# The scan's group statistics share the C.B bank, and the products' ring gets the bank set free

## The chip, the cores and the metric

The kernel runs on one core of a Trainium2 chip. The metric is the time of one execution in microseconds as the device counts it. The kernel before takes 2577.64 us, the median of three runs (2576.39 to 2583.05). The engines are called PE (TensorE, matmuls; PEld is its weight load), DVE (VectorE), ACT (ScalarE), POOL (GpSimd) and SP (SyncE, whose queue issues all the DMAs here). Each engine issues its own instructions in a fixed order and waits on semaphores for the others.

## The reference, cut to what matters

One layer of a streaming encoder works on 1088 tokens at once: 1024 of a new stream and 64 of a running one. The part around the change is this:

```python
xn = _rmsnorm(x, p['norm_mix_w'])
z, xbc, dt_raw, q, k, v, gate_ssm, gate_att = split(xn @ p['w_in'])
...
# the scan, chunk after chunk, 32 heads in 4 groups
cb = einsum('blgn,bsgn->blsg', cc, bc)
y = einsum('blsg,blsge,bsgep->blgep', cb, decay, xdt)
y = y + einsum('blgn,bgepn->blgep', cc, state) * exp(acum)
state = state * exp(acum[:, -1]) + einsum('blgn,blge,blgep->bgepn', bc, to_end, xdt)
...
y_ssm = (y + D * xs) * silu(z)
y_ssm = _rmsnorm(y_ssm per group, p['ssm_norm_w'])
o = diff_attention(q, k, v)
mix = sigmoid(gate_ssm) * (y_ssm @ w_branch_ssm) + sigmoid(gate_att) * (o @ w_branch_attn)
x = x + mix @ p['w_out']
x = x + conv_ffn(_rmsnorm(x))
```

## The kernel before, in words

Everything is kept transposed: features on the 128 partitions, tokens along the free axis. Tokens are cut in three columns of 384, 384 and 320 (`WIDE`). The stages follow each other: norm and values, q and k with their statistics, attention (with projections as filler), the scan (with projections and branches as filler), the rest of the branches, the output projection, the FFN.

**Products.** Every large matrix product runs in three passes over a high and a low part of both operands (`product`, lines 140 to 145), 24 matmuls for a product of eight k-tiles. The accumulator comes from `acc` (line 112), which hands out banks of PSUM in turn. During the first stage it turns over five banks, three of them from a pool that ends with that stage (`more`, line 226); from then on it has the two banks of the pool `pm`, tag "mm". A bank is free again when its reader has emptied it: for the branches that reader is the gate multiplication on VectorE (line 196, tile `b_g`). `project` (line 147) makes the tiles of the input projection; its accumulators are emptied by ScalarE. `branch` (line 156) makes a branch product: for each of the two halves of 544 tokens and each of eight output tiles it loads the gate and a weight tile, splits the weight in high and low (lines 136 and 137) and makes two products of 272 tokens. Where `stage` is given, it also loads the normed scan output in quarters (`b_f` from `y_sc`, line 168) and splits it into `b_hi` (ScalarE, line 169) and `b_lo` (VectorE, line 170). There are three branch calls: the attention's (768 matmuls), the scan's first two groups (768), and the scan's last two groups (768, after the scan).

**The scan.** It goes through 4 groups x 3 columns, 12 spans. A span has three steps of 128 tokens (the last step of the last column has 64). A step (`step`, from line 658) transposes x into `tr` (line 671), B and C.B into `cb` (lines 673 and 674), copies `cb` with ScalarE into `b_cb` (line 676), scales x on VectorE into `xdt` and `xw` (line 681), masks and exponentiates the decay on GpSimd and ScalarE (lines 682 and 684), multiplies it with C.B on VectorE (`bc`, line 685), and makes the within-chunk output `yi` (line 689), the carried-in output `ye` (line 696) and the state update `stp` (line 702). VectorE combines them (lines 697, 698 and 709). After a span's steps, `gated` adds D.x (line 718, VectorE), multiplies by the gate (line 719, GpSimd), squares (line 720, ScalarE), adds the four tiles up (lines 721 and 722, GpSimd), and one matmul with a matrix of ones sums over the partitions: the group sum, tile `gst` (line 724). From it `rstd_of` (lines 209 to 217) takes Ln and Exp on ScalarE and three more steps on VectorE, and line 728 scales y, which is then stored to `y_sc`.

**The banks in the scan.** PSUM has eight: two for `pm` ("mm"), and one each, with one buffer, for `tr`, `cb`, `yi`, `ye`, `stp` and `gst`. A tile of a one-buffer tag can be written only when all readers of the one before, in the program's order, are done.

**The order of the work.** The program is written as a scan that calls `fill` after each step and each `gated`: 2.5 filler units each time, first the rest of the input projection, from span 9 in the program's order on the branches. A scheduler that works with modelled durations then orders each engine's instructions before the program is built, so an instruction that would wait in the model is passed by later ones that would not, as far as buffers allow. What it decides is fixed on the chip.

Of the kernel before, what the change touches and what calls it, by code (L numbers as in the profile page):

```python
# [9 lines left out]
F32 = mybir.dt.float32  # L10
# [4 lines left out]
PSUM = bass.MemoryType.PSUM  # L15
DRAM = bass.MemoryType.DRAM

P = 128
# [58 lines left out]
def hybrid_layer(ctx: ExitStack, tc: tile.TileContext, xT, prm, cst, rope, wvd, win, wbs, wba, wout, wup, wdn,  # L77
# [27 lines left out]
    def col(o):  # L105
        return par[:, o : o + 1]

    pm = ctx.enter_context(tc.tile_pool(name="pm", bufs=2, space=PSUM))

    more, at_bank = None, 0  # L110

    def acc(w):
        nonlocal at_bank
        at_bank = (at_bank + 1) % 5
        pool, tag = (more, "mx") if more is not None and at_bank < 3 else (pm, "mm")
        t = pool.tile([P, 512], F32, name=tag, tag=tag)
        return t[:, :w]

# [28 lines left out]
    def project(block, evac):  # L147
        w_hi, w_lo = weights(block, KT, P)
        for c, w in WIDE:
            ps = acc(w)  # L150
            product(ps, [(w_hi[:, k], w_lo[:, k], xn_hi[:, k, c : c + w], xn_lo[:, k, c : c + w]) for k in range(KT)])
            with tc.high_priority(quick or ahead):
                evac(ps, c, w)
            yield

    def branch(stage, pair, src, wts, g0, add, out):
# [18 lines left out]
        for x, c in enumerate((0, HALF)):  # L175
            hi, lo = parts[x]
            if x == 0:
                parts[1] = octet()
            for m in range(KT):
                r = slice(P * m, P * (m + 1))  # L180
                two = pair()
                gt, at = two[:, :HALF], two[:, HALF:T]
                first = load(out=gt, in_=g_sc[g0 + P * m : g0 + P * (m + 1), c : c + HALF])
                if add is not None:
                    load(out=at, in_=add[r, c : c + HALF])
                w_hi, w_lo = weights(wts[m], KT, P)
                if x == 0 and m >= LAG:
                    with tc.issue_after(first.ins):
                        for k in range(8 * (m - LAG) // (8 - LAG), 8 * (m - LAG + 1) // (8 - LAG)):
                            bring(HALF, k, *parts[1])  # L190
                for a in (0, HALF // 2):
                    q = slice(a, a + HALF // 2)
                    ps = acc(HALF // 2)
                    product(ps, [(w_hi[:, k], w_lo[:, k], hi[:, k, q], lo[:, k, q]) for k in range(KT)])
                    with tc.high_priority(ahead):
                        V.scalar_tensor_tensor(gt[:, q], gt[:, q], 1.0, ps, ALU.add, ALU.mult)  # L196
                if add is not None:
                    V.tensor_tensor(out=gt, in0=gt, in1=at, op=ALU.add)
                out(m, c, gt)
                yield  # L200
# [4 lines left out]
    def run(gen):  # L205
        for _ in gen:
            pass

    def rstd_of(pool, out, mean, w, tag, scale=1.0, top=384):
        t = [pool.tile([P, top], F32, name=f"{tag}{i}", tag=f"{tag}{i}") for i in range(2)]  # L210
        u, r = (x[: out.shape[0], :w] for x in t)
        act(u, mean, AF.Ln, bias=eps_t[: out.shape[0]], scale=scale)
        act(r, u, AF.Exp, scale=-0.5)
        V.tensor_scalar(u, mean, -0.5 * scale, -0.5 * EPS, ALU.mult, ALU.add)
        V.tensor_tensor(out=u, in0=u, in1=r, op=ALU.mult)
        V.tensor_tensor(out=u, in0=u, in1=r, op=ALU.mult)
        V.scalar_tensor_tensor(out, u, 1.5, r, ALU.add, ALU.mult)
# [5 lines left out]

    s1 = ExitStack()
    ps1 = s1.enter_context(tc.tile_pool(name="ps1", bufs=1, space=PSUM))
    more = s1.enter_context(tc.tile_pool(name="psx", bufs=3, space=PSUM))

    def stat(w):
        t = ps1.tile([P, 512], F32, name="st", tag="st", bufs=3)
        return t[:, :w]  # L230
# [4 lines left out]
    with tc.tile_pool(name="nx", bufs=1) as nx:  # L235
        S.preload_act_table_set(LN_EXP)
        c = 0
        for x, w in enumerate(NORM):
            xc = nx.tile([P, KT, max(NORM)], F32, name="xc", tag="xc", bufs=3)
            ps = stat(w)  # L240
# [25 lines left out]
    def values(f, dt=None, pools=(None, None)):  # L266
        m = 256 if dt is None else 272
        w2 = [weights(win[B_V + 2 * f - 4 + u] if dt is None else wvd[2 * f + u], 4, m, pools[u]) for u in range(2)]
        for i in range(9):
            n = min(P, T - i * P)  # L270
            ps = acc(m)[:n]
            product(ps, [(xn_hi[:, k, P * i : P * i + n], xn_lo[:, k, P * i : P * i + n],
                          w2[k // 4][0][:, k % 4], w2[k // 4][1][:, k % 4]) for k in range(KT)])
            vo = staged("vo")[:, :256]
            with tc.high_priority(quick or ahead):
                S.copy(vo[:n], ps[:, :256])
                if dt is not None:
                    V.tensor_tensor(out=dt[:n, i, 16 * f : 16 * f + 16], in0=ps[:, 256:],
                                    in1=par[:n, O_DTB + 16 * f : O_DTB + 16 * f + 16], op=ALU.add)
            load(out=v[P * i : P * i + n, 256 * f : 256 * (f + 1)], in_=vo[:n])  # L280
            yield
# [124 lines left out]
            split_out(ck, j, PAST, c_st)  # L406
        heads(B_K, lambda j: col(O_KN + j), k_st, kT)
    s1.close()
    more = None
    ahead = AHEAD  # L410
    extra.release()
    extra = None
# [225 lines left out]


    with tc.tile_pool(name="sp", bufs=1) as sp, tc.tile_pool(name="pss", bufs=1, space=PSUM) as pss:  # L640
        def fetch(g, c, w):
            t = sp.tile([P, 10, 384], F32, name="in", tag="in", bufs=2)
            four = slice(4 * P * g, 4 * P * (g + 1))
            for u in range(2):
                load(out=t[:, u, :w], in_=x_sc[P * (16 + 4 * u + g) : P * (17 + 4 * u + g), c : c + w])
            for u, d in ((2, x_sc), (6, z_sc)):
                load(out=t[:, u : u + 4, :w], in_=d[four, c : c + w].rearrange("(j p) t -> p j t", p=P))
            return t
# [65 lines left out]
        def gated(g, c, w, xs, zt, y):  # L714
            rows = slice(4 * P * g, 4 * P * (g + 1))
            part = lambda d: d[rows, c : c + w].rearrange("(j p) t -> p j t", p=P)
            for j in range(4):
                V.scalar_tensor_tensor(y[:, j], xs[:, j, :w], col(O_D + 4 * g + j), y[:, j], ALU.mult, ALU.add)
            G.tensor_tensor(out=y, in0=y, in1=zt, op=ALU.mult)
            act(zt, y, AF.Square)  # L720
            G.tensor_tensor(out=zt[:, 0:2], in0=zt[:, 0:2], in1=zt[:, 2:4], op=ALU.add)
            G.tensor_tensor(out=zt[:, 0], in0=zt[:, 0], in1=zt[:, 1], op=ALU.add)
            ps = pss.tile([P, 512], F32, name="gst", tag="gst")[:, :w]
            PE.matmul(ps, ones, zt[:, 0], start=True, stop=True)
            rs = sp.tile([P, 384], F32, name="grs", tag="grs", bufs=2)[:, :w]
            rstd_of(sp, rs, ps, w, "gn", 1.0 / 512)
            for j in range(4):
                V.scalar_tensor_tensor(y[:, j], y[:, j], col(O_SN + 4 * g + j), rs, ALU.mult, ALU.mult)  # L728
            load(out=part(y_sc), in_=y)

        def scan():
            spans = [(g, c, w) for g in range(4) for c, w in WIDE]
            raw = fetch(*spans[0])
            ready = [gate(raw, spans[0][2])]
            for i, (g, c, w) in enumerate(spans):
                if c == 0:
                    state = None
                if i + 1 < len(spans):
                    raw = fetch(*spans[i + 1])
                bx, xs, zt = ready[i]  # L740
                y = sp.tile([P, 4, 384], F32, name="y", tag="y", bufs=2)
                for o in range(0, w, P):
                    state, last = step(g, (c + o) // P, o, bx, xs, y, state)
                    if o == P * GATE_AT and i + 1 < len(spans):
                        ready.append(gate(raw, spans[i + 1][2], last))
                    yield i
                gated(g, c, w, xs, zt, y[:, :, :w])
                yield i
# [21 lines left out]
            fill(SCAN_STEPS)  # L770
        load(out=conv, in_=conv_o)
        run(filler)
    dq.release()


# [17 lines left out]
    with tc.tile_pool(name="op", bufs=1) as op:  # L793
        for c, w in WIDE:
# [3 lines left out]
            for m in range(KT):  # L798
# [4 lines left out]
                ps = acc(w)  # L803
# [9 lines left out]
            ps = psf.tile([P, 512], F32, name="st2", tag="st2")[:, :w]  # L813
# [12 lines left out]
    with tc.tile_pool(name="fq", bufs=1) as fq, tc.tile_pool(name="fp", bufs=1) as fp:  # L826
# [42 lines left out]
        for n in DOWN:  # L869
            hid = [hidden(k0 + i) for i in range(n)]  # L870
            for mp2 in range(4):
                o = 1024 * k0 + 256 * n * mp2
                w_hi, w_lo = weights(wdn[:, o : o + 256 * n], n, 256)
                for u in range(2):
                    m = 2 * mp2 + u
                    for c, w in WIDE:
                        ps = acc(w)
# [114 lines left out]
```

## Time and profile before

| what | value |
|---|---|
| median of three runs | 2577.64 us |
| the profiled execution's own time | 2582.58 us |
| its span in the trace | 2580.8 us |
| norm, values, q and k | 0 to 416 us |
| attention | 416 to about 1116 us |
| scan, first transposes to last group sum | 1116.8 to 1567.0 us |
| rest of the branches, output projection, FFN | to 2580.8 us |

A row of stretches gives a length and each engine's busy time in it, with the number of instructions; then the granted clock of TensorE (1.00 is full), the DMA engines' share and GB/s. A row of groups names line, engine, operation, output and inputs, the count, then busy time and the mean of one in ns, then the idle time of the engine just before them and what ended it. A row of waits says who waited for whom: total us, times, longest.

### The profile page before, as it was taken

How to read it: one execution, taken by the hardware profiler on the slowest of the kernel's cores; microseconds unless marked ns; L12 is line 12 of the kernel's file. 1: busy time of each engine (PE TensorE's matmuls, PEld its weight loads, DVE VectorE, ACT ScalarE, POOL GpSimd, SP SyncE). 2: the span in 40 equal slices, each digit the busy share in tenths (PEclk: the TensorE clock that was granted, in tenths of full speed). 3: DMA queues.
4: the chain of work that ended last, by engine and by line, in shares of the span. 5: the costliest groups of instructions: out<-in, count | busy, mean ns of one | idle time of the engine just before them, and what ended most of it. 6: DMA issues, size and time to landing. Idle time of an engine off the chain costs nothing.

```text
span 2580.8 us, 41810 instructions
## 1 busy us (share of the span) xinstructions
PE 2525.0 (98%) x16484; PEld 2444.8 (95%) x16484; DVE 1399.8 (54%) x2371; ACT 1032.2 (40%) x2113; POOL 290.0 (11%) x387
## 2 busy tenths in 40 slices
PE   8999999999999999999999989999999999999999
PEld 7999999999999999988788879999999999999999
DVE  7326266654447674665679997658333333343333
ACT  5334234544445554565456643335312222131221
POOL 3000001000001110022333430023000000000000
PEclk9999999999999999999999999999999999999999
DMA  5217167545435433176798978555311111111112
GB/s 162 83 54 282 51 257 213 153 142 148 131 126 164 136 112 111 64 232 192 245 332 258 304 246 272 195 187 193 119 42 47 44 42 50 42 50 40 44 43 77
DMA packets 233685, 366.59 MB, mean 142 GB/s; under 512 B 31184, under 2 KB 160464, under 8 KB 233360
## 3 DMA queue, kind: packets, MB, share of 16 engines
q1 hardware_dynamic: 233488, 363.91, 44.2%
q8 instruction: 130, 2.13, 0.3%
q14 instruction: 67, 0.55, 0.1%
HBM read 263.56 MB, written 100.27 MB: 141 GB/s over the span
## 4 chain that ended last, share of the span: by engine, by line
PE 43%; DMA 3%; DVE 3%; ACT 1%; issue 1%; SPq 0%; POOL 0%; DVEq 0%; ACTq 0%; POOLq 0%
PE mm L143 7%; PE mm L145 7%; PE mm L144 7%; PE up L143 7%; PE up L145 7%; PE up L144 7%; DMA in<-x_sc 1%; DMA b_hi<-o_sc 1%; DVE w_lo L137 1%; PE yi L689 1%; PE stp L702 0%; ACT bc L684 0%; DVE y L728 0%; DMA in<-z_sc 0%; DVE b_lo L170 0%
## 5 line engine op out<-in xcount | busy, mean ns | idle before, releaser
L143 PE MATMUL mm<-xn_hi,w_hi 128*128 128x320 f32 (+1 forms) x1496 | 497.9, 333 | 2.3 <-ACT zr L428 1.1
L145 PE MATMUL mm<-xn_hi,w_lo 128*128 128x320 f32 (+1 forms) x1496 | 496.8, 332 | 0.0
L144 PE MATMUL mm<-xn_lo,w_hi 128*128 128x320 f32 (+1 forms) x1496 | 494.6, 331 | 0.0
L136 ACT CAST w_hi<-w_f 128x1024 fp32r<-128x1024 f32 (+2 forms) x220 | 229.3, 1042 | 547.2 <-PE mm L144 369.3
L137 DVE TENSOR_TENSOR w_lo<-w_f,w_hi 128x1024 fp32r<-128x1024 f32 (+2 forms) x220 | 284.9, 1295 | 300.8 <-ACT w_hi L136 298.4
L143 PE MATMUL up<-x_hi,w_hi 128*128 128x384 f32 (+1 forms) x1056 | 345.0, 327 | 2.7 <-ACT x_hi L820 2.7
L144 PE MATMUL up<-x_lo,w_hi 128*128 128x384 f32 (+1 forms) x1056 | 344.8, 327 | 0.0
L145 PE MATMUL up<-x_hi,w_lo 128*128 128x384 f32 (+1 forms) x1056 | 343.3, 327 | 0.0
L143 PEld LDWEIGHTS mm<-xn_hi,w_hi 128*128 128x128 f32 x1496 | 281.9, 188 | 7.9 <-issue 2.8
L145 PEld LDWEIGHTS mm<-xn_hi,w_lo 128*128 128x128 f32 x1496 | 281.6, 188 | 2.9 <-issue 1.9
L144 PEld LDWEIGHTS mm<-xn_lo,w_hi 128*128 128x128 f32 x1496 | 281.8, 188 | 2.6 <-issue 1.3
L143 PE MATMUL mm<-b_hi,w_hi 128*128 128x272 f32 x768 | 228.0, 298 | 19.1 <-DVE b_g L196 15.9
L144 PE MATMUL mm<-b_lo,w_hi 128*128 128x272 f32 x768 | 227.2, 296 | 0.7 <-DMA b_lo<-o_sc 0.7
L145 PE MATMUL mm<-b_hi,w_lo 128*128 128x272 f32 x768 | 227.5, 297 | 0.0
L143 PEld LDWEIGHTS up<-x_hi,w_hi 128*128 128x128 f32 x1056 | 198.7, 188 | 3.1 <-ACT x_hi L820 3.0
L144 PEld LDWEIGHTS up<-x_lo,w_hi 128*128 128x128 f32 x1056 | 198.8, 188 | 0.1
L145 PEld LDWEIGHTS up<-x_hi,w_lo 128*128 128x128 f32 x1056 | 198.5, 188 | 0.0
L880 DVE TENSOR_TENSOR xa<-xa,mm 128x384 f32<-128x384 f32 x144 | 76.5, 531 | 197.3 <-PE mm L145 197.3
L144 PE MATMUL mm<-f_lo,w_hi 128*128 128x384 f32 (+1 forms) x528 | 173.1, 328 | 0.0
L143 PE MATMUL mm<-f_hi,w_hi 128*128 128x384 f32 (+1 forms) x528 | 173.0, 328 | 0.0
L145 PE MATMUL mm<-f_hi,w_lo 128*128 128x384 f32 (+1 forms) x528 | 173.0, 328 | 0.0
L143 PEld LDWEIGHTS mm<-b_hi,w_hi 128*128 128x128 f32 x768 | 147.3, 192 | 25.4 <-DVE b_g L196 15.4
(252 smaller groups left out, 4803.7 us busy)
## 6 DMA issues: line engine op xcount, KB each, us to landing
w_f<-in_win_dram SPq DMA_DIRECT2D x76, 512.0 KB, 4.0
w_f<-in_wup_dram SPq DMA_DIRECT2D x44, 512.0 KB, 3.7
bc<-a_sc SPq DMA_DIRECT2D x32, 512.0 KB, 6.3
w_f<-in_wbs_dram SPq DMA_DIRECT2D x32, 512.0 KB, 4.2
b_g<-g_sc SPq DMA_DIRECT2D x48, 272.0 KB, 4.5
w_f<-in_wout_dram SPq DMA_DIRECT2D x24, 512.0 KB, 3.8
x_sc<-cc SPq DMA_DIRECT2D x48, 192.0 KB, 1.9
kh_t<-k_st SPq DMA_DIRECT2D x32, 272.0 KB, 6.9
```

Of the source, the lines that this page charges most:

```text
L136: S.copy(hi, w)
L137: V.tensor_tensor(out=lo, in0=w, in1=hi, op=ALU.subtract)
L143: PE.matmul(ps, a_hi, b_hi, start=i == 0, stop=False)
L144: PE.matmul(ps, a_hi, b_lo, start=False, stop=False)
L145: PE.matmul(ps, a_lo, b_hi, start=False, stop=i == n - 1)
L689: PE.matmul(yi[u : u + 64, e // 2, :L], xdt[:L, e], bc[:L, e, :L], start=True, stop=True)
L880: V.tensor_tensor(out=xa[:, m, c : c + w], in0=xa[:, m, c : c + w], in1=ps, op=ALU.add)
```

## The change

The group sum loses its own bank: its tile takes the tag "cb", whose single buffer it now shares with the steps' C.B, in the program's order. The bank set free goes to `acc`, which during the scan turns over three banks: one of the scan's pool (tag "mx") and the two of `pm`. `acc` now takes the number of extra banks from the pair `more`: three in the first stage, one in the scan, none elsewhere. No instruction is added, removed or given another size.

```diff
-    more, at_bank = None, 0
+    more, at_bank = (None, 0), 0
 
     def acc(w):
         nonlocal at_bank
-        at_bank = (at_bank + 1) % 5
-        pool, tag = (more, "mx") if more is not None and at_bank < 3 else (pm, "mm")
+        pool, n = more
+        at_bank = (at_bank + 1) % (n + 2)
+        pool, tag = (pool, "mx") if at_bank < n else (pm, "mm")
         t = pool.tile([P, 512], F32, name=tag, tag=tag)
         return t[:, :w]
...
-    more = s1.enter_context(tc.tile_pool(name="psx", bufs=3, space=PSUM))
+    more = s1.enter_context(tc.tile_pool(name="psx", bufs=3, space=PSUM)), 3
...
     s1.close()
-    more = None
+    more = None, 0
...
     with tc.tile_pool(name="sp", bufs=1) as sp, tc.tile_pool(name="pss", bufs=1, space=PSUM) as pss:
+        more = pss, 1
...
-            ps = pss.tile([P, 512], F32, name="gst", tag="gst")[:, :w]
+            ps = pss.tile([P, 512], F32, name="gst", tag="cb")[:, :w]
             PE.matmul(ps, ones, zt[:, 0], start=True, stop=True)
...
         run(filler)
+    more = None, 0
     dq.release()
```

## Prediction

> **What bounds the kernel now.** I read the page first, then the table of stretches, then TensorE's waits in the scan.
>
> ```profile
> span 2580.8 us, 41810 instructions
> PE 2525.0 (98%) x16484; PEld 2444.8 (95%) x16484; DVE 1399.8 (54%) x2371; ACT 1032.2 (40%) x2113; POOL 290.0 (11%) x387
> ```
>
> TensorE is busy for 2525.0 of 2580.8 us, so the change can give back at most what is lost between its instructions, and it touches the scan alone. The stretches (columns: length; PE, PEld, DVE, ACT, POOL busy; granted clock; DMA share; GB/s):
>
> ```profile
> 1100.00:1580.00 480.00, 445.31 (x3280) 400.43 (x3279) 368.85 (x525) 270.20 (x540) 167.42 (x114) 0.98 0.81 261
> 1375.00:1545.00 170.00, 152.92 (x1173) 135.64 (x1173) 157.86 (x222) 98.59 (x198) 66.87 (x41) 0.96 0.84 267
> 1580.00:1600.00 20.00, 20.00 (x161) 20.00 (x160) 10.12 (x17) 3.88 (x5) 0.00 (x0) 1.00 0.84 270
> ```
>
> The scan loses 480 - 445.3 = 34.7 us of TensorE. Half of it, 170 - 152.9 = 17.1 us, lies where VectorE is busy for 157.9 of 170 us. Behind the scan nothing is lost: 161 matmuls in 20 us, 0.124 us each; a product of 24 is 3 us. The waits in the scan (total, times, longest):
>
> ```profile
> PE mm L143 <- DVE b_g L196: 15.9, 8, 4.6
> PE tr L671 <- ACT in L653: 4.3, 5, 1.6
> ```
>
> The largest is the ring's: a product waits until VectorE has emptied one of two banks. The waits cost clock too:
>
> ```profile
> 1385.15 0.59 PE L143 MATMUL mm<-b_hi,w_hi 128*128 128x272 f32 x1 [4.58 <-DVE b_g L196]
> ...
> 1386.00:1388.00 2.00, 2.00 (x10) 2.00 (x10) 0.00 (x0) 0.00 (x0) 0.00 (x0) 0.50 0.76 227
> 1388.00:1390.00 2.00, 2.00 (x11) 2.00 (x10) 0.83 (x2) 0.00 (x0) 0.00 (x0) 0.50 0.37 146
> 1390.00:1392.00 2.00, 2.00 (x15) 2.00 (x14) 1.30 (x3) 0.00 (x0) 0.00 (x0) 0.77 0.00 0
> ```
>
> After 4.58 us without work the granted clock is 0.50 for some 6 us, which costs 3 us more. Over the 480 us the clock is 0.98: 0.02 x 445 is about 9 us. So the scan loses 34.7 + 9 = 43 us in all.
>
> **The change part by part.** No instruction is added or removed. Two things are tied differently, and the order in which the built program issues its instructions follows. Matmuls of products ahead of the first group sum, between each two, and behind the last, as TensorE issues them:
>
> ```
> before: 178 120 232 141 114 240 142 155 125 130 160 193 | 960
> after:  194 163 213 205 208 250 231 254 239 217  13  45 | 696
> ```
>
> (1) The ring. A third bank lets TensorE run one product, 3 us, further ahead of VectorE. At most the 15.9 us of ring waits go and their share of the clock. What would be late next are the other waits: 34.7 - 15.9 = 18.8 us, most of them steps that come late, like the transposes that wait for the silu on ScalarE. From the fourth group sum to the tenth the products lie more evenly than before (205 to 254 a span, not 114 to 240), which spreads the evictions over VectorE. I count half of the other waits as left, 10 us, with 5 us for the clock: 15 us lost in the first ten spans. It can't be seen in this trace; the ends are 5 us (little but the silu's 4.3 stays) and 30 us (VectorE, already 93% busy in 1375 to 1545, holds the ring as before).
>
> (2) The shared bank. It has one buffer, so the next span's first C.B transposes now wait until VectorE and ScalarE have read the group sum; behind them in TensorE's queue stand that span's steps and every later product. Before, those steps ran ahead of the sum. A group sum ends a long chain, D.x on VectorE, gate on GpSimd, square on ScalarE, two adds on GpSimd. The groups of the scan (busy, mean ns):
>
> ```profile
> L685 DVE TENSOR_TENSOR bc<-bc,b_cb 128x1024 f32<-128x1024 f32 (+1 forms) x36 | 51.6, 1434 | 7.0 <-ACT b_cb L676 6.4 <-ACT bc L684 0.5
> L728 DVE SCALAR_TENSOR_TENSOR y<-y,par,grs 128x384 f32<-128x384 f32 (+1 forms) x48 | 35.3, 794 | 0.4
> L170 DVE TENSOR_TENSOR b_lo<-b_f,b_hi 128x272 fp32r<-128x272 f32 x48 | 28.4, 618 | 3.9 <-ACT b_hi L169 3.9
> L718 DVE SCALAR_TENSOR_TENSOR y<-in,par,y 128x384 f32<-128x384 f32 (+1 forms) x48 | 27.6, 634 | 0.1
> L681 DVE TENSOR_TENSOR xdt<-tr,dt_tok 128x512 f32<-128x512 f32 (+1 forms) x36 | 24.6, 682 | 30.8 <-PE tr L671 30.7
> L709 DVE TENSOR_TENSOR state<-state,stp 128x512 f32<-128x512 f32 x32 | 21.7, 678 | 10.2 <-PE stp L702 5.4 <-POOL state L707 4.9
> L697 DVE TENSOR_TENSOR y<-ye,e 128x512 f32<-128x512 f32 (+1 forms) x32 | 20.7, 648 | 9.4 <-PE ye L696 7.9 <-DMA e<-e_sc 1.1 <-PE cb L673 0.4
> L698 DVE TENSOR_TENSOR y<-y,yi 128x512 f32<-128x512 f32 (+1 forms) x32 | 20.6, 644 | 5.4 <-PE yi L689 5.3
> L217 DVE SCALAR_TENSOR_TENSOR grs<-gn,gn 128x384 f32<-128x384 f32 (+1 forms) x12 | 8.4, 704 | 0.1
> L216 DVE TENSOR_TENSOR gn<-gn,gn 128x384 f32<-128x384 f32 (+1 forms) x12 | 7.2, 602 | 0.2
> L214 DVE TENSOR_SCALAR gn<-gst 128x384 f32<-128x384 f32 (+1 forms) x12 | 6.3, 527 | 2.8 <-ACT gn L213 2.7
> ```
>
> ```profile
> L169 ACT CAST b_hi<-b_f 128x272 fp32r<-128x272 f32 x48 | 18.6, 417 | 24.5 <-DMA b_f<-y_sc 21.7 <-PE mm L145 2.8
> L720 ACT ACTIVATE in<-y 128x1536 f32<-128x1536 f32 (+1 forms) x12 | 17.0, 1416 | 14.4 <-POOL y L719 14.4
> L212 ACT ACTIVATE gn<-gst,eps_t 128x384 f32<-128x384 f32 (+1 forms) x12 | 6.7, 560 | 10.6 <-PE gst L724 10.5
> L213 ACT ACTIVATE gn<-gn 128x384 f32<-128x384 f32 (+1 forms) x12 | 6.1, 507 | 0.2
> L676 ACT COPY b_cb<-cb 128x256 f32<-128x256 f32 (+1 forms) x36 | 12.9, 360 | 24.8 <-PE cb L674 20.7 <-PE stp L702 3.6 <-DVE bc L685 0.3
> L719 POOL TENSOR_TENSOR y<-y,in 128x1536 f32<-128x1536 f32 (+1 forms) x12 | 41.4, 3450 | 39.8 <-DVE y L718 33.7 <-ACT b_hi L169 6.2
> L721 POOL TENSOR_TENSOR in<-in 128x768 f32<-128x768 f32 (+1 forms) x12 | 22.8, 1899 | 10.1 <-ACT in L720 10.1
> L722 POOL TENSOR_TENSOR in<-in 128x384 f32<-128x384 f32 (+1 forms) x12 | 15.8, 1318 | 0.8
> ```
>
> In the first ten spans the wait is covered: 21 to 61 products stand between a group sum and the next C.B (36 are 4.5 us), while Ln, Exp and VectorE's read take 3 x 0.55 = 1.6 us, and a span's products (250 x 0.124 = 31 us) with its steps exceed its chain. If that cover went, it would be up to 3 us a span; the 30 us end holds it.
>
> (3) The tail. A longer scan eats more products: 2232 stand ahead of the last group sum, not 1930, and the second branch's run out at the tenth. The two last spans have 13 and 45 matmuls, 7 us, in place of 353, 44 us. The third branch can't fill in: its second half of rows needs these spans' output, stored and loaded again. So here the chain is bare. From the end of the tenth group sum, in VectorE's order:
>
> - Ln, Exp, VectorE's read 1.6; two more steps of rstd meanwhile the transposes and copy of C.B: 2.8 us.
> - C.B times decay 1.43, grs 0.70, state 0.68, four scalings 4 x 0.79, y 0.64: 9.4. The scaled y is stored from 8.8 on.
> - Second and third step, with three xdt/xw pairs (3 x 1.36), two C.B, two states, two carried-in and two added y (2 x (1.43 + 0.68 + 0.65 + 0.64)): 20.3, and 0.6 for a b_lo in VectorE's queue that needs the stored y: about 21, or as the store (6.7 us), load (4.6 us) and split allow.
> - D.x 4 x 0.63, gate 3.45, square 1.42, adds 1.90 + 1.32: 31 to 34; with hops and the sum itself 35.
>
> ```profile
> y_sc<-y SPq DMA_DIRECT2D x8, 768.0 KB, 6.7
> b_f<-y_sc SPq DMA_DIRECT2D x64, 136.0 KB, 4.6
> ```
>
> So the eleventh group sum ends 35 us after the tenth. From there the last span's first step has to come in again before VectorE reaches the scalings: 8.1 us; store and load 11.3; then seven b_hi/b_lo quarters at 0.62 behind each other, with 4 us of the step's own work between: 28 us. Only then, 63 us after the tenth sum, do the third branch's products stream. In these 63 us TensorE has six steps and 31 matmuls:
>
> ```profile
> 1272.62 0.60 PE L671 MATMUL tr<-con,in 128*128 128x128 f32 x4
> 1273.91 1.09 PE L689 MATMUL yi<-bc,xdt 128*64 128x128 f32 x16
> 1274.93 0.33 PE L673 MATMUL cb<-con,in 128*128 128x128 f32 x1
> 1275.10 0.39 PE L674 MATMUL cb<-in 128*128 128x128 f32 x2
> 1275.32 1.06 PE L696 MATMUL ye<-in,state 128*128 128x128 f32 x8
> 1276.95 1.02 PE L702 MATMUL stp<-xw,b_cb 128*128 128x512 f32 x2
> ```
>
> Six times 1.09 + 1.06 + 1.02 and 0.6 for C.B, three transposes, 31 x 0.124: about 27 us. Lost: 63 - 27 = 36 us. The clock adds: TensorE's pieces on the chain at half speed, about 3 us, and 6 us at half speed on restart, 3 us. **42 us**, between 30 (chain at VectorE's speed without GpSimd beside it) and 55 (store and load behind other transfers). By the Trainium skill ("TensorE: Matmul & The Clock Gate", Part 1: The HAM clock gate) the half rate comes after an idle window of about 3.4 us and goes after about 3.4 us of sustained work; the trace shows it after 4.58 us, lasting 6. By that rule the restart would cost an estimated 1.7 us, and the sum would be 1 us less.
>
> The last span's own store has 16 products of the first half, 48 us, as cover, and the output projection and FFN keep their order but for a few matmuls: nothing.
>
> The products that move ahead bring their DMAs with them: 302 matmuls are 13 products, some 6 weight loads of 512 KB more within the scan, at a DMA share of 0.81 there: nothing. SP issues in order, and its loads of the stored y hold what stands behind them, but in the tail nothing behind them could start earlier.
>
> ```profile
> 1566.30 0.70 PE L724 MATMUL gst<-in,con 128*128 128x320 f32 x2
> ```
>
> **The sum**: -43 + 15 + 42 = +14 us. The profiled execution took 2582.58 us (span 2580.8), 5 us over the median 2577.64; 2596.6 against its own time is **2592** against the median.
>
> **The rivals.** *The ring wins and the tail is short.* If the spans run even (5 us lost), and the tail at its low end (30), -43 + 35 = -8: 2570, faster. It decides where both together fall under 43 us; for it speaks that the ring's wait is the largest row, against it that the bare chain is nearly all VectorE and GpSimd time. *VectorE stays the bound.* In 1375 to 1545 it is 93% busy; a third bank is filled once and TensorE waits as before, now also for VectorE's read of the group sum: 30 lost, and a tail of 50: +37, 2615. A passage of the Trainium skill speaks for this (same page, "HAM oscillation — how this bites in real kernels"): there, double-buffering PSUM gave no further gain. No run here shows that yet. *Gain and cost cancel*, with 8 us in the spans and 36 in the tail: 2579. That the bank is not used at all is ruled out by the issue order, which puts products in it.
>
> **How the numbers follow.** The forecast (2583 to 2605) 0.50, VectorE as bound 0.16, cancelling 0.22, faster 0.12. About 0.3%, 7.7 us, is what a measurement of this kernel can tell from no change: faster 0.12, same 0.22, slower 0.66. The ends of the unknowns give -43 + 5 + 30 = -8 and -43 + 30 + 55 = +42; the range is 2570 to 2619.
>
> **What would show it.** Right: the wait of products on b_g under 8 us; the last group sum near 1566 - 43 + 15 + 302 x 0.124 + 42 = 1617 us, not 1566; TensorE idle for over 30 us between the tenth group sum and the third branch, at a clock near 0.5; the first ten spans under 25 us lost. Wrong: products between the last two group sums, a chain well under 30 us, or b_g waits as before.

## The result, and the profile after

The changed kernel takes **2613.68 us**, the median of four runs (2611.97 to 2617.31), beside 2578.36 us for the kernel before on the same chip: a ratio of 1.0139, 95% interval 1.0127 to 1.0151. It is 35 us slower. The forecast was 2592, 14 us slower: the sign was right and the time lies within the range, but 21 of the 35 us were not foreseen.

In the changed kernel the lines of the program stand one or two lower than before: the product is L144 to L146, the gate multiplication that empties a bank (`b_g`) L197, x's transposes L673, C.B L675 and L676, its copy `b_cb` L678, the state update L704, the group sum L726, its readers L213 and L215. The page's first rows, of the profiled execution (2617.31 us):

```profile
span 2615.5 us, 41796 instructions
PE 2538.2 (97%) x16484; PEld 2453.3 (94%) x16484; DVE 1384.8 (53%) x2371; ACT 1032.9 (39%) x2113; POOL 293.1 (11%) x387
```

As many matmuls, but 77.3 us between them where there were 55.8, and 13 us more inside them: the clock was lower in places. Three stretches of the scan show where, first those of the kernel before (columns as above: length; PE, PEld, DVE, ACT, POOL busy; granted clock; DMA share; GB/s):

```profile
1100.00:1130.00 30.00, 27.40 (x166) 26.00 (x165) 17.65 (x26) 19.33 (x38) 7.07 (x14) 1.00 0.91 300
1130.00:1570.00 440.00, 410.23 (x3059) 367.16 (x3058) 344.41 (x485) 247.93 (x498) 160.35 (x101) 0.98 0.81 258
1570.00:1660.00 90.00, 87.68 (x695) 87.27 (x694) 55.44 (x95) 29.03 (x45) 0.00 (x0) 1.00 0.71 234
```

and the same of the changed kernel, with the two stretches that the prediction's terms are about behind them:

```profile
1100.00:1130.00 30.00, 20.47 (x109) 18.45 (x107) 8.83 (x16) 12.90 (x22) 4.11 (x6) 0.89 0.90 292
1130.00:1570.00 440.00, 419.02 (x3122) 383.92 (x3122) 307.77 (x454) 239.01 (x475) 144.33 (x96) 0.98 0.79 254
1570.00:1660.00 90.00, 64.34 (x416) 52.59 (x415) 63.81 (x102) 33.34 (x66) 22.17 (x14) 0.77 0.51 166
...
1100.00:1570.00 470.00, 439.49 (x3230) 402.37 (x3228) 316.61 (x469) 251.92 (x495) 148.44 (x101) 0.97 0.80 257
1570.00:1638.00 68.00, 42.34 (x243) 30.67 (x241) 45.91 (x70) 24.69 (x52) 22.17 (x14) 0.70 0.47 153
```

TensorE idles 9.5 us in the first 30 us of the scan (2.6 before), 21.0 in the middle (29.8 before) and 25.7 in the tail (2.3 before), where its clock is 0.77 as well. So the middle did gain, 9 us. But the start lost 7 that nobody had counted, and the tail lost what had been forecast for it. TensorE's waits in the changed kernel (total us, times, longest), over the whole execution:

```profile
PE gst L726 <- POOL in L724: 18.9, 5, 10.4
PE stp L704 <- ACT b_cb L678: 12.6, 6, 6.0
PE tr L673 <- ACT in L655: 7.7, 1, 7.7
...
PE mm L145 <- DVE b_lo L171: 3.4, 1, 3.4
...
PE cb L675 <- DVE gn L215: 2.4, 2, 1.8
...
PE mx L144 <- DVE b_g L197: 0.6, 2, 0.3
PE mm L144 <- DVE b_g L197: 0.5, 1, 0.5
```

and the two first of them in the kernel before:

```profile
PE gst L724 <- POOL in L722: 1.5, 2, 0.9
PE stp L702 <- ACT b_cb L676: 1.2, 1, 1.2
```

The ring's wait on `b_g`, 15.9 us before, is down to 0.6 + 0.5 = 1.1 us. In its place the group sum waits for the adds on GpSimd, 18.9 us where it was 1.5, and the state update for the copy of C.B, 12.6 where it was 1.2. The wait went because TensorE had more to do ahead of it, and it came back as others, since the work behind it was no earlier. The first, the tenth and the last two group sums:

```profile
1170.21 1.65 PE L726 MATMUL gst<-in,con 128*128 128x384 f32 x2 [3.23 <-POOL in L724]
...
1569.61 0.81 PE L726 MATMUL gst<-in,con 128*128 128x384 f32 x2
...
1604.84 1.65 PE L726 MATMUL gst<-in,con 128*128 128x384 f32 x2 [10.41 <-POOL in L724]
...
1637.63 0.70 PE L726 MATMUL gst<-in,con 128*128 128x320 f32 x2
```

Nine spans in 399.4 us are 44.4 us each; the two bare ones behind them take 35.2 and 32.8 (the last has a shorter third step). This is the number to keep in mind: a span whose chain must end before the next begins costs 44 us while VectorE and TensorE also work on branches, and 35 without. In the kernel before, where spans overlap, the first ten sums lie 36.5 us apart (1167.46 to 1495.59).

### The profile page after: what moved, and what is told of

It is laid out like the page before. It is cut to its first block, busy times and chain, and to the rows that moved or that the text cites. A ratio compares the mean times of both kernels' runs of the same rounds, so it can differ in the third digit from the quotient of the medians.

```text
span 2615.5 us, 41796 instructions
## 1 busy us (share of the span) xinstructions
PE 2538.2 (97%) x16484; PEld 2453.3 (94%) x16484; DVE 1384.8 (53%) x2371; ACT 1032.9 (39%) x2113; POOL 293.1 (11%) x387
## 4 chain that ended last, share of the span: by engine, by line
PE 43%; DMA 4%; DVE 4%; ACT 2%; issue 2%; POOL 1%; SPq 0%; DVEq 0%; ACTq 0%; POOLq 0%
PE up L144 7%; PE up L146 7%; PE up L145 7%; PE mm L144 7%; PE mm L146 6%; PE mm L145 6%; DMA in<-x_sc 2%; PE stp L704 1%; PE yi L691 1%; DVE w_lo L138 1%; DMA bc<-a_sc 1%; PE mx L146 1%; PE ye L698 0%; PE mx L145 0%; PE mx L144 0%
## 5 line engine op out<-in xcount | busy, mean ns | idle before, releaser
L144 PE MATMUL mm<-xn_hi,w_hi 128*128 128x384 f32 (+1 forms) x1416 | 470.5, 332 | 0.0
L146 PE MATMUL mm<-xn_hi,w_lo 128*128 128x384 f32 (+1 forms) x1416 | 468.0, 331 | 0.0
L145 PE MATMUL mm<-xn_lo,w_hi 128*128 128x384 f32 (+1 forms) x1416 | 466.9, 330 | 0.0
L144 PE MATMUL up<-x_hi,w_hi 128*128 128x384 f32 (+1 forms) x1056 | 345.1, 327 | 2.5 <-ACT x_hi L823 2.5
L146 PE MATMUL up<-x_hi,w_lo 128*128 128x384 f32 (+1 forms) x1056 | 343.0, 327 | 0.0
L144 PEld LDWEIGHTS mm<-xn_hi,w_hi 128*128 128x128 f32 x1416 | 266.8, 188 | 3.6 <-issue 1.8
L145 PEld LDWEIGHTS mm<-xn_lo,w_hi 128*128 128x128 f32 x1416 | 266.9, 188 | 1.9 <-issue 0.7
L146 PEld LDWEIGHTS mm<-xn_hi,w_lo 128*128 128x128 f32 x1416 | 266.7, 188 | 1.1 <-issue 0.2
L144 PEld LDWEIGHTS up<-x_hi,w_hi 128*128 128x128 f32 x1056 | 198.7, 188 | 2.9 <-ACT x_hi L823 2.8
L146 PEld LDWEIGHTS up<-x_hi,w_lo 128*128 128x128 f32 x1056 | 198.4, 188 | 0.0
L145 PE MATMUL mm<-b_lo,w_hi 128*128 128x272 f32 x592 | 174.7, 295 | 3.4 <-DVE b_lo L171 3.4
L144 PE MATMUL mm<-b_hi,w_hi 128*128 128x272 f32 x592 | 175.5, 298 | 1.3 <-ACT zr L429 0.8
L146 PE MATMUL mm<-b_hi,w_lo 128*128 128x272 f32 x592 | 174.9, 296 | 0.8 <-DVE w_lo L138 0.7
L144 PE MATMUL mm<-f_hi,w_hi 128*128 128x384 f32 (+1 forms) x528 | 173.0, 328 | 0.0
L146 PE MATMUL mm<-f_hi,w_lo 128*128 128x384 f32 (+1 forms) x528 | 172.9, 328 | 0.0
L458 DVE SCALAR_TENSOR_TENSOR cc<-pre,par,cc 128x384 f32<-128x384 f32 (+1 forms) x216 | 128.6, 598 | 43.0 <-ACT cc L456 39.2
```

The lines of the kernel that those rows point to most:

```text
L144: PE.matmul(ps, a_hi, b_hi, start=i == 0, stop=False)
L145: PE.matmul(ps, a_hi, b_lo, start=False, stop=False)
L146: PE.matmul(ps, a_lo, b_hi, start=False, stop=i == n - 1)
L458: V.scalar_tensor_tensor(cc[:, :m], pre[:, i : i + m], cw(i), cc[:, :m], ALU.mult, ALU.add)
```

## The experiments

The runs come in the order of the argument. Each ratio is to the kernel before, timed on the same chip, with its 95% interval. "TensorE idle" is the length less the busy time in the three stretches above.

| kernel | median us | ratio | idle 1100 to 1130 | 1130 to 1570 | 1570 to 1660 |
|---|---|---|---|---|---|
| before | 2578.36 | | 2.6 | 29.8 | 2.3 |
| changed | 2613.68 | 1.0139 | 9.5 | 21.0 | 25.7 |
| share_alone | 2605.71 | 1.0100 | 2.8 | 26.8 | 19.7 |
| ring_from_span_2 | 2607.37 | 1.0103 | 2.2 | 26.2 | 22.5 |
| sum_in_yi_bank | 2595.03 | 1.0054 | 7.8 | 28.9 | 3.5 |
| shared_even | 2630.20 | 1.0191 | 7.1 | 51.4 | 11.2 |
| shared_even_ring_from_span_2 | 2612.69 | 1.0117 | 2.3 | 47.9 | 8.6 |
| before_queued | 2593.16 | 1.0049 | 2.7 | 31.4 | 5.6 |
| before_chained | 2593.71 | 1.0059 | 2.4 | 31.5 | 8.6 |
| shared_two_buffers | 2591.48 | 1.0043 | 2.1 | 28.6 | 6.0 |

### One half of the change at a time

**share_alone**: the group sum shares C.B's bank, and the products keep two.

```diff
-        more = pss, 1
+        more = None, 0
```

> The group sum shares the C.B bank as in the changed kernel; the products keep two banks and the bank set free stays empty. Theory (the sharing makes the spans a chain, which spends the products early and leaves the last two spans bare, 39 us in the trace of the changed kernel): the tail stays, the late first transposes (about 13 us with their clock) go, the ring's waits (16 us and their clock) come back: 2605 to 2620 us. Rival (the third bank is what costs, because its products can't run before attention has released its banks): 2575 to 2590 us, like before.

2605.71 us, 1.0100 (1.008 to 1.012), so by the ratios 26 of the 36 us come from sharing alone, and the third bank adds 10 where it should have given. Its waits:

```profile
PE mm L144 <- DVE b_g L197: 12.4, 8, 5.1
PE gst L726 <- POOL in L724: 7.8, 2, 7.6
...
PE stp L704 <- ACT b_cb L678: 3.3, 4, 1.4
```

The ring waits are back, 12.4 us, and the waits for GpSimd and for the copy are down from 18.9 to 7.8 and from 12.6 to 3.3: the one kind is exchanged for the other.

**ring_from_span_2**: the changed kernel, but `acc` gets the third bank only when the second span begins.

```diff
-        more = pss, 1
...
+                if i == 1:
+                    more = pss, 1
```

> The changed kernel, but the third bank joins the products' ring only from the second span in the program's order, so that no product that covers the end of attention is bound to it. Theory: the idle time of 1100 to 1120 us (7.7 us wait for the silu, and its clock) goes, the tail stays: 2600 us, 6 either way. Rival (the third bank costs throughout, or nothing at the start): 2613 us as the changed kernel. If the third bank at the start were the whole of the loss: under 2585 us.

2607.37 us, 1.0103 (1.0082 to 1.0123): some 7 us slower than expected, and 9 us faster than the changed kernel by the ratios. The loss at the start is gone (idle 2.2 us of the first 30, clock 1.00). In the middle it idles 26.2 us, as share_alone does with two banks (26.8):

```profile
PE gst L725 <- POOL in L723: 14.3, 4, 9.4
PE stp L703 <- ACT b_cb L677: 7.5, 7, 2.4
```

With the third bank 12.4 us of ring waits went to 3.1, and the waits for the group sum and the copy grew by 10.7. In this kernel the third bank is worth nothing.

**sum_in_yi_bank** and **sum_in_yi_bank_two**: the group sum shares the bank of `yi` instead, the step's third piece of work, with three banks for the products and, the second (with share_alone's line as well), with two.

```diff
-            ps = pss.tile([P, 512], F32, name="gst", tag="cb")[:, :w]
+            ps = pss.tile([P, 512], F32, name="gst", tag="yi")[:, :w]
```

> The changed kernel, but the group sum shares the bank of yi (the within-chunk output, later in a step than C.B), so the next span's transposes, C.B and decay product need not wait for it; three banks for products. As issued, 167 to 201 matmuls of products stand ahead of each of the last two group sums, not 13 and 45. Theory (the loss is the bare tail): about 39 us less than the changed kernel, 2570 to 2585 us. Rival (the third bank costs, or VectorE is the bound): 2600 to 2613 us.

> As the run with the sum in yi's bank, but two banks for products, the third stays empty. Theory (a third bank wins the ring's waits, some 15 us, and loses some 13 at the start of the scan): 2572 to 2590 us, within 8 us of the run with three. Rival (the third bank is harmful): 15 us or more under the run with three. If the ring alone is worth its 16 us without loss: 15 us or more above it.

2595.03 us, 1.0054 (1.0037 to 1.0071), between the two expectations; and with two banks 2583.15 us, 1.0013 (0.9998 to 1.0027), no change that can be told. So that two tiles share a bank costs nothing here; it costs with **C.B as the partner**, the first thing that a span needs. The idle time of the first behind 1570 is 3.5 us: no bare tail.

**sum_in_yi_bank_ring_from_span_2**: both together.

> The group sum in yi's bank, the third bank in the ring from the second span on. Against the run with yi's bank and three banks throughout (2595 us) this takes the start away: 2581 to 2587 us if the start is all that the third bank costs there. Against the run with two banks (2583 us) it shows the ring by itself: under 2575 us if the ring's 16 us of waits were real time on TensorE, 2579 to 2587 us if other waits take their place.

2580.47 us, 0.9993 (0.9983 to 1.0004). Here the third bank is worth 0.2% by the ratios (2580.47 beside 2583.15 us), which the overlapping intervals don't tell from nothing, and having it from the first span on costs 0.6% (1.0054 against 0.9993). This is the best version that leaves nothing out, and it can't be told from the kernel before.

That the loss at the start comes with the third bank is shown by these runs; how it comes is read from the diff and the trace. The third bank belongs to the scan's pool, which opens over banks that attention still uses, so products that `acc` has given it wait until attention has let go of its bank: in the changed kernel the first of them starts at 1105.4 us, attention's last transposes at 1101.1. So 38 of TensorE's instructions less stand ahead of the scan's first transposes, and these then wait 7.7 us for a silu of ScalarE with nothing left to cover it.

### Is it only the bare tail?

My first theory after the result was that the tail's 25.7 us are the whole cost, and that the middle would give up products at no price. **shared_even** issues the branches' products, from the fourth tile on, behind a named group sum, so that they spread over all spans (matmuls ahead of each sum: 194 163 213 198 192 144 192 192 144 192 192 214, where the changed kernel has 13 and 45 at the end).

```diff
+    held = iter((None, None, None, 3, 3, 3, 3, 4, 4, 4, 5, 5, 5, 5, 6, 6, 6, 6, 7, 7, 7, 8, 8, 8, 8, 9, 9, 9, 9, 10, 10, 10))
...
+                behind = next(held, None)
...
-                    product(ps, [(w_hi[:, k], w_lo[:, k], hi[:, k, q], lo[:, k, q]) for k in range(KT)])
+                    with tc.issue_after(sums[behind].ins) if behind is not None else ExitStack():
+                        product(ps, [(w_hi[:, k], w_lo[:, k], hi[:, k, q], lo[:, k, q]) for k in range(KT)])
...
-            PE.matmul(ps, ones, zt[:, 0], start=True, stop=True)
+            sums.append(PE.matmul(ps, ones, zt[:, 0], start=True, stop=True))
```

> The changed kernel with one thing added: each branch product from the fourth on is issued behind a named group sum, so that the products lie evenly (144 to 214 matmuls ahead of each sum, also the last two) instead of being used up by the tenth. Bank sharing and ring as in the changed kernel. Theory (the sharing costs because the early spans take the products and leave the tail bare; tail 39 us in the trace): the tail's idle time goes, part of it comes back in the spans, whose products (192 x 0.124 = 24 us) with three steps (13 us) then just exceed the chain of 35 us: 2580 to 2597 us. Rival (the chain from sum to sum is itself the bound, wherever the products lie): 2605 to 2615 us, the idle time spread over the spans.

2630.20 us, 1.0191 (1.0174 to 1.0209): slower than either expectation, and than the changed kernel. The theory fell. The first rows of its waits (the profiled execution took 2638.27 us, 8 over the median):

```profile
PE gst L731 <- POOL in L729: 42.5, 9, 10.4
PE stp L709 <- ACT b_cb L683: 12.5, 4, 3.9
```

The tail idles 11.2 us instead of 25.7, but the middle 51.4 instead of 21.0. Its twelve sums lie 44.1 us apart (1173.6 to 1658.6), as far as in the changed kernel's first ten spans (44.4): with some 35 matmuls of products less in each of the first ten spans (1824 ahead of the tenth sum, not 2174) a span is no shorter, and TensorE waits for GpSimd's adds instead. So with a shared bank TensorE's work alone doesn't set a span's length; the chain from sum to sum, with what lies on it, does. The changed kernel's middle is full only because it uses up the products that the last spans then lack.

**shared_even_ring_from_span_2** gives it the third bank from the second span on (both diffs above).

> As shared_even, and the third bank joins the ring only from the second span on. Theory (start of the scan and tail are two separate losses that add up): 6 to 10 us less than shared_even. Rival (they are one and the same, products lost at the start are won later): the same as shared_even within 3 us.

2612.69 us, 1.0117 (1.0101 to 1.0132): 17.5 us less than shared_even, more than expected. By the profiles 5 of them are idle time at the start (7.1 to 2.3), 3.5 in the middle and 2.6 in the tail; I have no cause for more than the start, and shared_even's profiled execution was itself 8 us above the median.

**shared_until_span_8** shares C.B's bank in the first eight spans and `yi`'s in the last four, to keep products for the end.

```diff
-            ps = pss.tile([P, 512], F32, name="gst", tag="cb")[:, :w]
+            ps = pss.tile([P, 512], F32, name="gst", tag="cb" if 3 * g + (c > 0) + (c > 384) < 8 else "yi")[:, :w]
```

> The changed kernel, but the last four group sums take yi's bank instead of C.B's; the order of issue leaves 67 and 45 matmuls ahead of the last two sums, as in the changed kernel nearly. Theory (the tail is bare because the earlier, shared spans used the products): 2600 to 2613 us, the sharing in the tail itself matters little. Rival (what costs in the tail is the wait of C.B for the sum): 2575 to 2590 us.

2615.51 us, 1.0126 (1.0112 to 1.0140), above what was expected. It kept nothing: the last two spans have 67 and 45 matmuls of products. It speaks against its rival (2575 to 2590 us): once the early spans have used the products up, taking the last four sums out of C.B's bank gives nothing back. It doesn't tell the chain from the bare tail.

### The chain, shortened

If the chain sets the pace, a shorter chain must give time back in each span. Three kernels leave out the two adds on GpSimd, so that the group statistics cover one tile of four; their times are read with that.

```diff
-            G.tensor_tensor(out=zt[:, 0:2], in0=zt[:, 0:2], in1=zt[:, 2:4], op=ALU.add)
-            G.tensor_tensor(out=zt[:, 0], in0=zt[:, 0], in1=zt[:, 1], op=ALU.add)
```

> As shared_even, but GpSimd's two adds ahead of the group sum are left out (the sum then takes one of its four tiles), which takes 3.2 us out of the chain from one group sum to the next and leaves the products where they were (182 to 192 a span). Theory now (since C.B waits for the sum, the twelve spans are one chain, and the chain, not the products, sets the scan): the seven spans that waited for the sum and the two behind them each get 3 us or more shorter: 2590 to 2608 us. Rival (the first theory: what counts is where the products lie): 2620 us or more.

> The changed kernel with the two adds left out (the sum takes one of its four tiles). As issued, the last two sums then have 144 and 51 matmuls ahead, not 13 and 45. Theory (chain): every span gets shorter and fewer products are used up early: 2573 to 2593 us. Rival (only the bare tail counts, two spans of 3.2 us): 2604 to 2610 us.

> The kernel before with the same two adds left out, as a control. There the next span's steps run ahead of the sum, so the chain is not closed: theory: 2572 to 2580 us, 8 us or less gained. If it gains as much as the changed kernel does, the adds cost for another reason (GpSimd slowing VectorE) and the control takes that off.

shared_even_no_adds: 2599.51 us, 1.0057 (1.0039 to 1.0076), down by 1.34%, 35 us. Its twelve sums go from 1164.6 to 1613.9, 449.3 us in place of 485.0: 35.7 / 11 = 3.25 us a span, and the adds take 1.90 + 1.32 = 3.22 in the groups of the kernel before. That the two agree so closely is in part luck: shared_even's profiled execution is 8 us above its median, the other's 3.6 below. changed_no_adds: 2591.91 us, 1.0035 (1.0022 to 1.0047), down by 1.04%, 27 us; with 144 and 51 matmuls left to its last two spans it idles 10.2 us behind 1570, not 25.7. But before_no_adds, the control: 2567.08 us, 0.9929 (0.9911 to 0.9948), down by 0.71%, 18 us, and more than was expected. Between kernels without the adds the change costs 1.0035 / 0.9929 = 1.0107, against 1.0139 with them: the adds are a part of the price of the change, the larger part stays.

A rival stands beside the chain, and the control's expectation had named it: GpSimd's adds may slow VectorE. The trace of the kernel before shows it. A `b_lo`, which takes 0.43 us in the median, takes 2.08 here, from 0.24 us after an add has begun to 0.3 us after the add's end:

```profile
1431.55 2.02 POOL L721 TENSOR_TENSOR in<-in 128x768 f32<-128x768 f32 x1
1431.79 2.08 DVE L170 TENSOR_TENSOR b_lo<-b_f,b_hi 128x272 fp32r<-128x272 f32 x1
```

Between 1130 and 1660 us the instructions of VectorE that run beside an add take, added up, some 14 us more than the shortest of their form in the kernel before, some 8 in the changed kernel and 10 in shared_even. So the control's 18 us may be VectorE's as much as the chain's, and of shared_even's 35 us up to about 10 may be. The experiment shows what the adds cost, not that they cost it as links of the chain alone.

### What of sharing costs: the order, the readers, the bank

**before_queued** is the kernel before, each tile in its own bank, with the first C.B transposes of a span issued behind the group sum of the one before. Only the order is changed.

```diff
-            PE.transpose(cb[:L, 0:P], bx[:, 0, cs], ident)
-            PE.matmul(cb[:L, P : P + L], bx[:, 0, cs], bx[:, 1, cs], start=True, stop=True)
+            with tc.issue_after(sums[-1].ins) if sums and o == 0 else ExitStack():
+                PE.transpose(cb[:L, 0:P], bx[:, 0, cs], ident)
+                PE.matmul(cb[:L, P : P + L], bx[:, 0, cs], bx[:, 1, cs], start=True, stop=True)
...
```

> The kernel before, with its own bank for the group sum and two for products, and one thing added: the first C.B transposes of a span are issued behind the group sum of the span before (order of issue alone, no shared bank). As issued, 233 and 128 matmuls of products stand ahead of the last two sums, so the tail isn't bare. Theory (the closed chain from sum to sum costs, by whatever it is closed): the sums come 40 to 44 us apart, and 2597 to 2612 us, near the 2606 us of the shared bank alone. Rival (the shared bank itself, or the bare tail, costs, not the order): 2578 to 2590 us.

2593.16 us, 1.0049 (1.0031 to 1.0067), between the two expectations: half of share_alone's cost comes with the order alone, without a shared bank. Spans that overlapped, 36.5 us apart, now follow each other, 40.3 us apart over the first ten sums (1171.0 to 1533.3).

**before_chained** adds the readers' part by order: the copy of C.B behind Exp on ScalarE, the decay product behind VectorE's read. `reads` holds the two instructions that `rstd_of` returns.

```diff
-            S.copy(b_cb[:L, : P + L], cb[:L, : P + L])
+            with tc.issue_after(reads[-1][0].ins) if reads and o == 0 else ExitStack():
+                S.copy(b_cb[:L, : P + L], cb[:L, : P + L])
...
```

> The kernel before with its own bank for each, and by order of issue alone the waits of a shared bank: C.B's transposes behind the group sum of the span before (as before_queued), and also the copy of the decayed C.B behind Exp's read and the decay product behind VectorE's read of the group sum. Theory (the other half of what share_alone lost is the wait for the readers of the sum): 2602 to 2610. Rival (that half lies in the bare tail, where the two kernels have different products left): 2589 to 2597, as before_queued with 2593.16.

2593.71 us, 1.0059 (1.0038 to 1.0079): what the rival expected. The readers on the other engines cost nothing more that can be told. What it lacks of share_alone is the tail: 8.6 us idle behind 1570, not 19.7, with 220 and 114 matmuls of products in the last spans, not 37 and 45.

**shared_two_buffers** shares, but a tag of two banks: the free bank stays with the pair instead of going to the products.

```diff
-            cb = pss.tile([P, 512], F32, name="cb", tag="cb")
+            cb = pss.tile([P, 512], F32, name="cb", tag="cb", bufs=2)
...
-            ps = pss.tile([P, 512], F32, name="gst", tag="gst")[:, :w]
+            ps = pss.tile([P, 512], F32, name="gst", tag="cb", bufs=2)[:, :w]
```

> Group sum and C.B share one tag, but a tag of two banks (the bank set free stays with them), and the products keep two. A product of C.B then takes the bank that the second last of the pair left, so C.B of a span no longer waits for the readers of the sum before it. Theory (what costs is the one bank, in which every first user waits for the last reader of the other): within 0.5% of the kernel before, 2570 to 2590. Rival (the order of issue that a shared tag brings is what costs, one bank or two): 2597 to 2606, as share_alone with 2605.71.

2591.48 us, 1.0043 (1.0028 to 1.0059), 1.5 us above the theory's bound and 5 below the rival's: between them, and level with before_queued, whose order it nearly has. The traces agree: in both kernels C.B starts right behind the sum (once 1.4 us later), and the first ten sums lie 40.2 and 40.3 us apart. So with two buffers the order is left to pay, and the other half comes with the single bank, in which C.B can start only when VectorE has read the sum.

How that wait grows can be read off the trace. In the changed kernel, between the seventh group sum and the next C.B, with the C.B behind the eleventh as the last row:

```profile
1429.70 0.91 PE L726 MATMUL gst<-in,con 128*128 128x384 f32 x2 [0.68 <-POOL in L724]
...
1433.42 0.56 DVE L215 TENSOR_SCALAR gn<-gst 128x384 f32<-128x384 f32 x1
...
1434.97 0.27 PE L675 MATMUL cb<-con,in 128*128 128x128 f32 x1
...
1608.31 0.47 PE L675 MATMUL cb<-con,in 128*128 128x128 f32 x1 [1.82 <-DVE gn L215]
```

and in before_chained:

```profile
1404.13 0.81 PE L730 MATMUL gst<-in,con 128*128 128x384 f32 x2
...
1404.78 0.27 PE L677 MATMUL cb<-con,in 128*128 128x128 f32 x1
```

There C.B comes right behind the sum. In the changed kernel it comes 4.36 us after the sum's end at 1430.61, though in the bare tail C.B waits 1.82 us for VectorE's read. In between TensorE works without a gap on 34 matmuls of products. Two things lengthen the wait. Here it is mostly the read itself, which ends at 1433.98, 3.37 us after the sum, since ScalarE's and VectorE's work for the branches lies ahead of it. In the other eight gaps of the first ten spans the read has ended 1.6 to 2.4 us after the sum, and C.B follows it only 2.4 to 5.3 us later, behind products: the order of issue that has them in the wait is fixed, and they are longer than it. In share_alone the gap is 3.6 to 6.4 us in the first ten spans, and its sums lie 43.0 us apart there, not 40.3. The longer spans take in 2112 matmuls of products ahead of the tenth sum, before_queued's 1828; the 284 more, 35 us of work at 0.124, are what the tail lacks. That these matmuls, and not the wait for the read alone, lengthen the span is argued from the rows; no run takes them out of the gap and leaves the shared bank.

## Why the prediction was wrong in size

**The failed step is (1), the 15 us lost in the first ten spans.** They lost 470 - 439.5 = 30.5 us and 0.03 x 439 = 13 of clock, 43 in all: as much as the whole scan had lost before, and beyond the upper end of 30. Three parts of it:

- *The ring's waits go, with their clock.* They went (15.9 to 1.1, under the 8 that were asked), but not their time. The step counted the other waits as fixed and halved them; share_alone and ring_from_span_2 show them growing as the ring's shrink. The rival had the right outcome, a third bank that is worth nothing, with the wrong engine: VectorE was busy for 308 of 440 us in the middle, less than before (344).
- *The cover in (2).* "A span's products with its steps exceed its chain" is where it failed. The chain was added up from bare durations, 35 us, and bare spans do take 35.2 and 32.8. In the first ten spans it takes 44.4. The products that stand between sum and C.B (27 to 45 in the trace's nine gaps, where 21 to 61 were named) were counted as cover for the wait; by the rows above they lie on the chain themselves. And where products are few, as in shared_even, TensorE waits for the chain for 42.5 us.
- *The start*, 7 us of idle time and clock 0.89 in 30 us, was in no term. The diff points to the reason: the third bank comes from a pool that opens when attention's closes. The issue order showed it too, in 38 instructions less ahead of the first transposes. I read the products' counts from the first group sum on, and not what stands ahead of it.

**Term (3), the tail, was right**: 42 us forecast, 68 - 42.3 = 25.7 of idle time and 0.30 x 42.3 = 13 of clock measured, 38.5. The eleventh sum came 35.2 us after the tenth (35 forecast), the third branch's stream 1629.55 - 1569.61 = 60 us after it (63). The end of the chain, which was forecast as D.x, gate, square and two adds, in the changed kernel:

```profile
1593.61 2.82 DVE L720 SCALAR_TENSOR_TENSOR y<-in,par,y 128x384 f32<-128x384 f32 x4
...
1596.92 3.41 POOL L721 TENSOR_TENSOR y<-y,in 128x1536 f32<-128x1536 f32 x1
...
1600.36 1.48 ACT L722 ACTIVATE in<-y 128x1536 f32<-128x1536 f32 x1 [1.37 <-POOL y L721]
...
1601.92 1.80 POOL L723 TENSOR_TENSOR in<-in 128x768 f32<-128x768 f32 x1 [1.59 <-ACT in L722]
...
1603.80 0.99 POOL L724 TENSOR_TENSOR in<-in 128x384 f32<-128x384 f32 x1
```

From D.x's end at 1596.4 it is 8.4 us to the eleventh group sum at 1604.84, and TensorE has nothing in all of them. How the 42 are made up was less exact: "over 30 us idle at a clock near 0.5" was asked, and it is 25.7 at 0.70, since TensorE's own pieces, many at half speed, take 34.4 us to the third branch's stream (1570 to 1629.5) and not 27. The terms that the prediction lists for them add up to 28.3.

**The sum**: -43 + 15 + 42 = 14 became -43 + 43 + 38 = 38, against 34.7 between the two spans; the clock in the rows has two digits, and 0.01 of 500 us is 5 us. The last group sum came at 1637.6, not 1617: 20 us later, since (1) was short by 28 and (3) too long by 4, less 4 that the reckoning leaves open. The rival that gave 2615 had the time, by way of 30 us in the spans and 50 in the tail, neither of which is what came. Of the signs of being wrong, none appeared. Of those of being right, the wait on `b_g` came; "the first ten spans under 25 us lost" failed, and with it the time of the last group sum and, in part, the tail's idle time and clock.

The passage of the Trainium skill on double-buffering PSUM ("TensorE: Matmul & The Clock Gate", "HAM oscillation — how this bites in real kernels") was weighed as a rival. It is about two banks in place of one; here a third beside two gave nothing that can be told either: 2605.71 us without it and 2607.37 with it (share_alone, ring_from_span_2), 2583.15 and 2580.47 with the sum in `yi`'s bank.

What stays open: the 17.5 us between shared_even's two forms, how far the second half of sharing's cost is the wait and how far the products inside it, and how much of the adds' cost is the chain's and how much VectorE's. A version with the adds off GpSimd, to which before_no_adds points (0.71% there), was not tried.

## What to carry to other kernels

When a buffer is shared, look at which of the next round's users comes first: shared with the head of a chain it closes a loop from round to round, while shared with a later link it was free. Work that is put into a wait to cover it can come to lie on the chain itself, and work that is used up early is missing at the end; so compare the whole loop's length, as the trace shows it with everything beside it, to the work that is there for each round. A wait that is removed is a gain only if the next one, with the row that shows it, can't take its place.

## What the runs showed of the hardware

The half clock after a wait can last longer than the wait. In the kernel before, the ring's wait of 4.58 us (the row at 1385.15 in the prediction) is followed by 5.81 us of unbroken matmuls at half clock, which cost 2.9 us:

```profile
1385.15:1390.96 5.81, 5.81 (x25) 5.81 (x26) 1.58 (x3) 0.00 (x0) 0.00 (x0) 0.50 0.57 158
```

In the changed kernel the stream of the third branch's products starts after a wait of 3.42 us, with the clock at 0.50 already since 1620:

```profile
1629.55 0.59 PE L145 MATMUL mm<-b_lo,w_hi 128*128 128x272 f32 x1 [3.42 <-DVE b_lo L171]
1629.94 0.43 PE L146 MATMUL mm<-b_hi,w_lo 128*128 128x272 f32 x1
1630.17 0.43 PE L144 MATMUL mm<-b_hi,w_hi 128*128 128x272 f32 x1
...
1632.04 0.59 PE L144 MATMUL mm<-b_hi,w_hi 128*128 128x272 f32 x1 [0.53 <-DVE b_g L197]
...
1637.12 0.29 PE L146 MATMUL mm<-b_hi,w_lo 128*128 128x272 f32 x1
1637.25 0.29 PE L144 MATMUL mm<-b_hi,w_hi 128*128 128x272 f32 x1
```

The starts are 0.23 us apart until past 1636, and then 0.13: behind the one break, 0.53 us at 1632, it is 4.7 us of unbroken matmuls at half speed. The Trainium skill ("TensorE: Matmul & The Clock Gate", "Part 1: The HAM clock gate") has the half rate end after about 3.4 us of sustained work; these rows show 5.8 and 4.7.

The other surprise is the weight of two small adds on an engine that is 11% busy: without them the kernel before is 0.71% (0.52 to 0.89) faster. The rows above show one way in which they weigh: a VectorE instruction of 0.43 us takes 2.08 beside one of them.
